# A Hymba block's up projection on one core: the weight rows read into buffers of half a row, each taken anew by itself, and the last stores put on three queues

## The chip, the core and the metric

One core of a Trainium2 chip runs the kernel. The metric is the device time of one launch in microseconds (us); smaller is better. The engines named below are PE (matrix products), DVE and ACT (elementwise work), POOL (here almost only an issuer of transfers) and SP (issues transfers and nothing else). Each engine works through its own instructions in a fixed order. An instruction whose inputs are not ready holds up everything behind it on that engine, and a transfer that must wait for its buffer holds up the transfers behind it on the same queue.

## The reference, cut to what matters

The block is one decoder layer on 512 tokens of width 2048: an input projection, two token mixers, an output projection, and then a gated feed-forward part. The change touches this last part and the final norm:

```
h = rmsnorm(x) * (1 + sc2) + sh2                       # 512 x 2048
u = h @ w_up                                           # 2048 -> 2 * 5632
y = conv_b + sum_j conv_w[j] * shifted(u, j)           # causal, width 3
val, gate = split(y)
x = x + gt2 * ((silu(gate) * val) @ w_down)
return rmsnorm(x)
```

## The kernel before

All large products are made in three passes (`mm3`, lines 118 to 122): each operand is split into a rounded part and a remainder, and hi*hi, hi*lo and lo*hi are added. For the weights, `wsplit` (line 845) does it on the fly: ACT casts 128x1024 numbers to the high part (line 850), and DVE subtracts to get the low part `ulo` (line 852). Three pairs of buffers are used in turn, so a cast may begin only when the product three places earlier has used its high part up.

**The steps of the up projection.** The 88 output tiles of 128 channels are taken as 44 pairs (a value tile and its gate tile), one pair a step `j`. The pair's weights are two rows of `wup`, 128x2048 each (1 MB). With the input channels cut in two, a row gives two parts: row `2j` is W11 and W12, row `2j+1` is W21 and W22. The activations are cut into two input halves and two token halves. Each step is then a product of two 2x2 block matrices and is made of seven block products of 24 matmuls each (128x128 by 128x256) in the place of eight. Their weights are, in the program's order:

| product | weight | activation tiles (PE rows) |
|---|---|---|
| 1 | w11 | y (Y11) |
| 2 | w12 | y (Y21) |
| 3 | r1 = W21 + W22 | t (T1) |
| 4 | r2 = r1 + w11 | t (T2) |
| 5 | r4 = r2 + w12 | y (Y22) |
| 6 | r3 = W11 + W21 | t (T3) |
| 7 | w22 | t (T4), made a step later |

DVE makes `r2` and `r4` by additions (lines 1022 and 1030). `r1` and `r3` are made by transfers: SP loads one addend, and POOL then issues an accumulating transfer that adds the other on top (lines 995 and 998). `r2`, `r3` and `r4` use the three `wide` buffers.

**The order of the steps.** For the first ten pairs, products 1 and 2 were already made ahead of the loop (`first_two`) and stored in `early`. The loop goes 10, 0, 11, 1, ..., 19, 9 and then 20 to 43. A step with `j >= 10` makes seven products on PE (its own first six, and product 7 of the step before); I call it a full step. A step with `j < 10` (`NB` in the code) makes five; I call it a short step. So the first twenty steps are ten pairs of a full and a short step with 12 products, and the last 24 are full steps.

**The row buffers.** Four buffers of 1 MB (tags `x2_0` to `x2_3`) hold the rows. Every step takes two of them, and two steps later they are taken again:

```python
w.append(row(2 * j + i, rb, f"x2_{(0, 2, 1, 3)[rows % 4]}"))
...
w11, w12, r1, w22 = w[0][:, W1], w[0][:, W2], w[1][:, W1], w[1][:, W2]
G.dma_start(r1, a["wup"][2 * j + 1, :, W2], accum_op=ALU.add)
```

A row is one tile and is loaded by one transfer of 1 MB (line 865). The second row holds W21, on which `r1` is accumulated, and W22, whose product is made only in the following step; the tile is given back when both have been read.

**What sets the order on the engines.** The program is written in the order above, but a scheduler then places the instructions of each engine. For the trace it is its placing that counts.

**The end.** After the down projection, the last residual gives a norm over the second 256 tokens. Four blocks of 128x4x256 (512 KB each) are multiplied by it and stored (`finish`, line 1132): the first on POOL, the other three on DVE, and all four stores stand on SP's queue, the first block's ahead.

Of the kernel before, what the change touches and what calls it, by code (L numbers as in the profile page):

```python
# [9 lines left out]
F32 = mybir.dt.float32  # L10
# [6 lines left out]
P = 128  # L17
# [9 lines left out]
NB = 10  # L27
# [28 lines left out]
def block_kernel(ctx, tc, a, out, stop=None, dbg=None):  # L56
    nc = tc.nc
    V, S, G, PE = nc.vector, nc.scalar, nc.gpsimd, nc.tensor
# [118 lines left out]
    if True:  # L177
# [9 lines left out]
        rstd = p0.tile([P, T], F32, tag="rs0", name="rs0")  # L187
# [18 lines left out]
        for k in range(KT):  # L206
            for part in (1, 0):
                j = part * 16 + k
                wa = p0.tile([P, D], F32, tag="wa", name="wa", bufs=4)
# [405 lines left out]
    def start_pair(p):  # L615
        if p:
            rkv = []
            for i in range(3):
                t = vtile("v") if i == 2 else ring("rkv")
                nc.sync.dma_start(t, sp[p, i])  # L620
                rkv.append(t)
        else:
            rkv = rkv0
        return stage_a(p, rkv)
# [5 lines left out]
    with hp():  # L630
        q = start_pair(0)
        stage_b(0, q)
    win_pair(1)
    for p in range(NP):
# [5 lines left out]
        with hp():  # L640
            stage_c(p, q)
            if p + 1 < NP:
                stage_b(p + 1, qn)
                q = qn
# [51 lines left out]
    rb = ctx.enter_context(tc.tile_pool(name="rb", bufs=1, reuse_waits="tile"))  # L696
    psm = ctx.enter_context(tc.tile_pool(name="psm", bufs=8, space=PSUM, reuse_waits="tile"))
    HT = T // 2
    H0, H1 = slice(0, HT), slice(HT, T)
    QW = 4 * P  # L700

    def bank():
        return psm.tile([P, T], F32, tag="b", name="b")
# [5 lines left out]
    def wide(name):  # L709

        return rb.tile([P, 4, HT], F32, tag="wide", name=name, bufs=3)
# [31 lines left out]
    def norm_rows(acc):  # L743
        pst = bank()
        rms_stats(pst, acc)
        return rms_rows(rb, pst, HT // P)

    def norm_bcast(dg):
        psb = bank()
        rms_bcast(psb, dg, HT // P)  # L750
        return psb[:, 0:HT]
# [52 lines left out]
    for f in range(8, KT):  # L804
        if f == 9:
            dg = norm_rows(acc[:, H0])
        if f == 10:
            rstd = norm_bcast(dg)
# [46 lines left out]
    def product(ps, w, Y, start=True):  # L855
        wh, wl = wsplit(w)
        for k in range(8):
            sl = slice(k * P, (k + 1) * P)
            y = Y[k // 4]
            mm3(ps, wh[:, sl], wl[:, sl], y[:, 0, k % 4, :], y[:, 1, k % 4, :], start=start and k == 0,  # L860
                stop=k == 7, more=not start)

    def row(n, pool, tag):
        t = pool.tile([P, 4 * QW], F32, tag=tag, name="wrow")
        nc.sync.dma_start(t, a["wup"][n, :, :])
        return t

    W1, W2 = slice(0, 2 * QW), slice(2 * QW, 4 * QW)
# [42 lines left out]
    for n in range(NB):  # L911
# [3 lines left out]
        if n == 1:  # L915
            rstd = norm_bcast(dg)
# [21 lines left out]
    def finish_pair(j, u1, u2):  # L938
        yv, yg = Slot("yv"), Slot("yg")
        conv(u1.t, yv.t, col("cw", j), col("cw", 88 + j), col("cw", 176 + j), col("cb", j))  # L940
        u1.done()

        conv(u2.t, yg.t, ncw[:, 0, j : j + 1], ncw[:, 1, j : j + 1], ncw[:, 2, j : j + 1], col("cb", 44 + j))
        u2.done()
        S.activation(yg.t, yg.t, AF.Silu)
        V.tensor_mul(yv.t, yv.t, yg.t)
        yg.done()
        nc.sync.dma_start(ad[j], yv.t)
        yv.done()
# [4 lines left out]
    def act_pair(i):  # L954

        pool, tag = ATAGS[i % len(ATAGS)]
        t = pool.tile([P, 2, 2, T], F32R, tag=tag, name="act2")
        for n in range(2):
            s_ = Slot("al")
            nc.sync.dma_start(s_.t, ad[2 * i + n])  # L960
            S.copy(t[:, 0, n, :], s_.t)
            V.tensor_tensor(t[:, 1, n, :], s_.t, t[:, 0, n, :].bitcast(F32), op=ALU.subtract)
            s_.done()
        return [(t[:, 0, n, :], t[:, 1, n, :]) for n in range(2)]
# [3 lines left out]
    def ahead_of_down(j):  # L968
        if j == NF - 1:
            A.extend(act_pair(len(A) // 2))  # L970

    pend = None

    def last_product(p):

        j, u1, u2, b, w22, x = p
        product(b, w22, T4, start=False)
        if x is None:
            S.copy(u2[:, H0], b)
        else:  # L980
            V.tensor_add(u2[:, H0], x[:, H0], b)
            x.done()
        finish_pair(j, u1, u2)


    order = [j for n in range(NB) for j in (NB + n, n)] + list(range(2 * NB, NF))
    rows = 0
    for j in order:
        w = []
        for i in range(2):  # L990
            w.append(row(2 * j + i, rb, f"x2_{(0, 2, 1, 3)[rows % 4]}"))
            rows += 1

        w11, w12, r1, w22 = w[0][:, W1], w[0][:, W2], w[1][:, W1], w[1][:, W2]
        G.dma_start(r1, a["wup"][2 * j + 1, :, W2], accum_op=ALU.add)
        r3 = wide("r3").rearrange("p a b -> p (a b)")
        nc.sync.dma_start(r3, a["wup"][2 * j, :, W1])
        G.dma_start(r3, a["wup"][2 * j + 1, :, W1], accum_op=ALU.add)
        pa = bank()[:, 0:HT]
        cap = Slot("cap")  # L1000
        if j < NB:
            u1 = Slot("u1")
            nc.sync.dma_start(u1.t, early[j])
            if pend:
                last_product(pend)
        else:
            product(pa, w11, Y11)
            S.copy(cap[:, H0], pa)
            if pend:
                last_product(pend)  # L1010
            u1 = Slot("u1")
            pb = bank()[:, 0:HT]
            product(pb, w12, Y21)
            V.tensor_add(u1[:, H0], cap[:, H0], pb)
        ahead_of_down(j)
        u2 = Slot("u2")
        pc = bank()[:, 0:HT]
        product(pc, r1, T1)
        S.copy(cap[:, H1], pc)
        ahead_of_down(j)  # L1020
        r2 = wide("r2").rearrange("p a b -> p (a b)")
        V.tensor_add(r2, r1, w11)
        product(pa, r2, T2, start=j < NB)
        if j < NB:
            V.tensor_add(cap[:, H0], u1[:, H1], pa)
        else:
            S.copy(cap[:, H0], pa)
        ahead_of_down(j)
        r4 = wide("r4").rearrange("p a b -> p (a b)")
        V.tensor_add(r4, r2, w12)  # L1030
        product(pc, r4, Y22, start=False)
        V.tensor_add(u1[:, H1], cap[:, H0], pc)
        ahead_of_down(j)
        if j < NB:
            pd = bank()[:, 0:HT]
            product(pd, r3, T3)
            V.tensor_add(u2[:, H1], cap[:, H0], cap[:, H1])
            V.tensor_add(u2[:, H1], u2[:, H1], pd)
            pend = (j, u1, u2, pd, w22, cap)
        else:  # L1040
            product(pa, r3, T3, start=False)
            V.tensor_add(u2[:, H1], cap[:, H1], pa)  # L1042
            cap.done()
            pend = (j, u1, u2, pa, w22, None)
# [84 lines left out]
        residual(f, ps, gate(f), acc, lo, hi, f == 0)  # L1129
        S.activation(x2(f, slice(lo, hi)), x2(f, slice(lo, hi)), AF.Identity, bias=eps[:, 2:3], scale=col("nf", f))  # L1130

    def finish(hs, q, rstd, eng=V):
        x = x2q[q][:, :, hs]
        eng.tensor_tensor(x, x, rstd[:, None, :].to_broadcast([P, 4, HT]), op=ALU.mult)
        nc.sync.dma_start(out[:, 4 * q : 4 * q + 4, hs], x)

    for f in range(NWF):
        if f == 0:
# [9 lines left out]
    for f in range(NWF, KT):  # L1148
        n = f - NWF
        if n == 1:  # L1150
            dg = norm_rows(acc[:, H0])
        if n == 2:
            rstd = norm_bcast(dg)
        if n >= 3 and n < 7:
            finish(H0, n - 3, rstd)
        down_half(1, f)
    rstd = norm_bcast(norm_rows(acc[:, H1]))
    rs = Slot("rs")
    S.copy(rs[:, H0], rstd)
    finish(H1, 0, rs[:, H0], G)  # L1160
    for q in range(1, 4):
        finish(H1, q, rstd)


def pack(x, c, w_ada, b_ada, norm1_g, w_in, mu_shift, w0, w2, a0, a2, g2, k_k, k_a, r_k, ln_x_w, ln_x_b,
# [95 lines left out]
```

## Time and profile before

| | us |
|---|---|
| median of 3 runs | 2437.19 (2434.59 to 2441.55) |
| the profiled execution's own time | 2435.95 |
| its span, from the first to the last instruction | 2434.2 |
| PE busy | 2299.5 (94% of the span) |
| DVE busy | 1643.5 (68%) |
| ACT busy | 1058.0 (43%) |
| mean clock granted to PE | 0.982 |

In the profile's rows, a line such as L852 is a line of the kernel, `out<-in` names the tiles with their numbers left out (`wrow` is a weight row, `r` any of r2, r3 and r4, `u` a result), and `x` is a count. The bracket at the end of a row is how long the engine stood idle just before it and what it was waiting for. A row of SPq or POOL with DMA_DIRECT2D is the issue of a transfer, not the transfer itself. PEclk is the clock granted to PE as a share of its full one, and DMA is the mean busy share of the core's 16 transfer engines. The up projection's loop lies between about 1040 and 1900 us of the span, and its ten pairs of steps end near 1440.

### The profile page before, as it was taken

Reading aid. Unit: us, or ns where it says so; the run is one execution under the profiler, and the core shown is the slowest. Engines: PE = TensorE matmul, PEld = TensorE weight load, DVE = VectorE, ACT = ScalarE, POOL = GpSimd, SP = SyncE. Lnnn points to the kernel's source line nnn. Section 1 sums busy time; section 2 is a strip of 40 time slices with the busy share of each in tenths; the row PEclk is TensorE's granted clock in tenths of the full one; section 3 lists DMA queues with packets and bytes.
Section 4 is the critical chain, followed back from the end, with each engine's and each line's share of the span. In section 5 each row is a group of like instructions: output and inputs, shape, how many; then the busy total and the mean of one; then the engine's idle time right before and its main releaser. Section 6 shows DMA issues by size and latency. Waiting matters only on the chain.

```text
span 2434.2 us, 42678 instructions
## 1 busy us (share of the span) xinstructions
PE 2299.5 (94%) x17122; PEld 1990.3 (82%) x17122; DVE 1643.5 (68%) x2623; ACT 1058.0 (43%) x1491; POOL 127.0 (5%) x184
## 2 busy tenths in 40 slices
PE   4789999999999999999989899999999999999997
PEld 3656666667666789999989899999999988888897
DVE  6987777777774456776767677777777735353354
ACT  3234344443433346644444445555555622233353
POOL 0000000000000010011010000000001000110000
PEclk9999999999999999999999999999999999999998
DMA  9976665556572756677676777677777857764465
GB/s 343 340 230 164 169 166 152 166 168 176 166 209 74 251 180 185 219 225 208 201 204 201 207 199 196 197 200 202 200 199 203 255 172 280 249 205 119 115 181 162
DMA packets 213946, 483.06 MB, mean 198 GB/s; under 512 B 73137, under 2 KB 78705, under 8 KB 194289
## 3 DMA queue, kind: packets, MB, share of 16 engines
q1 hardware_dynamic: 195026, 414.77, 52.4%
q0 software_dynamic: 18720, 65.55, 13.1%
q8 instruction: 134, 2.20, 0.4%
q14 instruction: 66, 0.54, 0.1%
HBM read 441.70 MB, written 38.54 MB: 197 GB/s over the span
## 4 chain that ended last, share of the span: by engine, by line
PE 73%; DMA 10%; DVE 9%; issue 3%; ACT 3%; SPq 1%; DVEq 0%; POOLq 0%; ACTq 0%
PE b L122 17%; PE b L120 17%; PE b L121 17%; DMA wrow<-wup 7%; PE mm L120 3%; PE mm L121 3%; PE mm L122 3%; DVE jk L212 3%; DVE ulo L852 2%; PE pb L537 1%; PE pb L535 1%; DMA war<-ada 1%; PE pb L528 1%; DMA wraw<-win 1%; DVE wlo L115 1%
## 5 line engine op out<-in xcount | busy, mean ns | idle before, releaser
L122 PE MATMUL b<-t,ulo 128*128 128x256 f32 x1408 | 403.5, 288 | 34.3 <-DVE ulo L852 34.3
L120 PE MATMUL b<-t,uhi 128*128 128x256 f32 x1408 | 403.5, 287 | 0.9 <-DVE u L1042 0.9
L121 PE MATMUL b<-t,uhi 128*128 128x256 f32 x1408 | 402.3, 286 | 0.0
L122 PE MATMUL b<-act,ulo 128*128 128x512 f32 (+1 forms) x880 | 308.0, 350 | 0.0
L121 PE MATMUL b<-act,uhi 128*128 128x512 f32 (+1 forms) x880 | 307.8, 350 | 0.0
L120 PE MATMUL b<-act,uhi 128*128 128x512 f32 (+1 forms) x880 | 307.6, 350 | 0.0
L122 PEld LDWEIGHTS b<-t,ulo 128*128 128x128 f32 x1408 | 272.4, 194 | 36.9 <-DVE ulo L852 36.9
L120 PE MATMUL b<-y,uhi 128*128 128x256 f32 x1056 | 299.1, 283 | 1.0 <-ACT uhi L850 1.0
L122 PE MATMUL b<-y,ulo 128*128 128x256 f32 x1056 | 298.5, 283 | 0.7 <-DVE ulo L852 0.7
L121 PE MATMUL b<-y,uhi 128*128 128x256 f32 x1056 | 298.5, 283 | 0.0
L850 ACT CAST uhi<-wrow 128x1024 fp32r<-128x1024 f32 x176 | 184.4, 1048 | 226.9 <-PE b L121 214.8
L852 DVE TENSOR_TENSOR ulo<-wd,uhi 128x1024 fp32r<-128x1024 f32 (+1 forms) x120 | 136.3, 1135 | 215.8 <-ACT uhi L850 215.0
L120 PEld LDWEIGHTS b<-t,uhi 128*128 128x128 f32 x1408 | 272.8, 194 | 2.4 <-DVE u L1042 1.3
L121 PEld LDWEIGHTS b<-t,uhi 128*128 128x128 f32 x1408 | 272.6, 194 | 0.0
L113 ACT CAST whi<-wraw 128x512 fp32r<-128x512 f32 x236 | 145.6, 619 | 286.4 <-PE mm L121 114.3
L852 DVE TENSOR_TENSOR ulo<-wrow,uhi 128x1024 fp32r<-128x1024 f32 x176 | 214.7, 1222 | 69.8 <-ACT uhi L850 69.8
L850 ACT CAST uhi<-wd 128x1024 fp32r<-128x1024 f32 (+1 forms) x120 | 117.4, 978 | 292.4 <-PE b L121 290.7
L115 DVE TENSOR_TENSOR wlo<-wraw,whi 128x512 fp32r<-128x512 f32 x236 | 161.4, 688 | 113.9 <-ACT whi L113 101.3
L852 DVE TENSOR_TENSOR ulo<-r,uhi 128x1024 fp32r<-128x1024 f32 x132 | 161.1, 1220 | 72.7 <-ACT uhi L850 72.4
L850 ACT CAST uhi<-r 128x1024 fp32r<-128x1024 f32 x132 | 138.6, 1050 | 161.6 <-PE b L121 160.1
L120 PEld LDWEIGHTS b<-y,uhi 128*128 128x128 f32 x1056 | 201.5, 191 | 1.4 <-ACT uhi L850 1.4
L122 PEld LDWEIGHTS b<-y,ulo 128*128 128x128 f32 x1056 | 200.8, 190 | 1.1 <-DVE ulo L852 1.1
(310 smaller groups left out, 4706.3 us busy)
## 6 DMA issues: line engine op xcount, KB each, us to landing
wrow<-wup SPq DMA_DIRECT2D x98, 1024.0 KB, 5.3
wa<-ada SPq DMA_DIRECT2D x48, 1024.0 KB, 7.1
war<-ada SPq DMA_DIRECT2D x192, 256.0 KB, 3.5
wd<-wdn SPq DMA_DIRECT2D x80, 512.0 KB, 4.0
wraw<-win SPq DMA_DIRECT2D x140, 256.0 KB, 4.2
wraw<-wout SPq DMA_DIRECT2D x96, 256.0 KB, 3.5
wrow<-wup POOLq DMA_DIRECT2D x44, 512.0 KB, 5.7
r<-wup SPq DMA_DIRECT2D x44, 512.0 KB, 4.6
```

What stands on the lines that cost most here:

```text
L113: S.copy(hi, raw)
L115: eng.tensor_tensor(lo, raw, hi[:, :].bitcast(F32), op=ALU.subtract)
L120: PE.matmul(ps, wh, xh, start=start, stop=False, skip_group_check=more)
L121: PE.matmul(ps, wh, xl, start=False, stop=False, skip_group_check=more)
L122: return PE.matmul(ps, wl, xh, start=False, stop=stop, skip_group_check=more)
L212: V.scalar_tensor_tensor(jk, wa, 1.0, cb, op0=ALU.mult, op1=ALU.mult, accum_out=mod[:, j : j + 1])
L528: PE.transpose(pst[:, i * P : (i + 1) * P], src[:, cl], ident)
L535: PE.matmul(pss[h][:, 0:128], bt[HS[h], cl], ar[HS[h], c, 1, :], start=True, stop=True)
L537: PE.matmul(pss[h][:, 128:384], kt[HS[h], cl], ar[HS[h], c, :, :], start=True, stop=True)
L850: S.copy(hi[:, 0:n], src)
L852: lo_of[0] = V.tensor_tensor(lo[:, 0:n], src, hi[:, 0:n].bitcast(F32), op=ALU.subtract)
```

## The change

The four buffers of 1 MB are taken once, ahead of the loop, and each is used as two halves; a half is a quarter of a step's weights, hence `wquart`. Each half is loaded by a transfer of its own, and waits only for the readers of its own earlier contents. The parts are paired anew: W21 (which becomes r1) shares a buffer with w11, and w12 one with w22. W21 is written first in the program. In a short step, product 7 of the step before is written after the product of r1 and no longer before it. Two of the last four stores go to ACT's queue, one to POOL's, and one stays with SP.

```diff
-    rows = 0
-    for j in order:
-        w = []
-        for i in range(2):
-            w.append(row(2 * j + i, rb, f"x2_{(0, 2, 1, 3)[rows % 4]}"))
-            rows += 1
-
-        w11, w12, r1, w22 = w[0][:, W1], w[0][:, W2], w[1][:, W1], w[1][:, W2]
+    wq = [rb.tile([P, 4 * QW], F32, tag=f"x2_{i}", name="wquart") for i in (0, 2, 1, 3)]
+    for n, j in enumerate(order):
+        wa, wb = wq[2 * (n % 2)], wq[2 * (n % 2) + 1]
+
+        r1, w11, w12, w22 = wa[:, W1], wa[:, W2], wb[:, W1], wb[:, W2]
+        nc.sync.dma_start(r1, a["wup"][2 * j + 1, :, W1])
         G.dma_start(r1, a["wup"][2 * j + 1, :, W2], accum_op=ALU.add)
+        nc.sync.dma_start(w11, a["wup"][2 * j, :, W1])
+        nc.sync.dma_start(w12, a["wup"][2 * j, :, W2])
+        nc.sync.dma_start(w22, a["wup"][2 * j + 1, :, W2])
         r3 = wide("r3").rearrange("p a b -> p (a b)")
         nc.sync.dma_start(r3, a["wup"][2 * j, :, W1])
         G.dma_start(r3, a["wup"][2 * j + 1, :, W1], accum_op=ALU.add)
...
         if j < NB:
             u1 = Slot("u1")
             nc.sync.dma_start(u1.t, early[j])
-            if pend:
-                last_product(pend)
...
         product(pc, r1, T1)
         S.copy(cap[:, H1], pc)
+        if j < NB:
+            last_product(pend)
...
-    def finish(hs, q, rstd, eng=V):
+    def finish(hs, q, rstd, eng=V, store=nc.sync):
         x = x2q[q][:, :, hs]
         eng.tensor_tensor(x, x, rstd[:, None, :].to_broadcast([P, 4, HT]), op=ALU.mult)
-        nc.sync.dma_start(out[:, 4 * q : 4 * q + 4, hs], x)
+        store.dma_start(out[:, 4 * q : 4 * q + 4, hs], x)
...
-    finish(H1, 0, rs[:, H0], G)
+    finish(H1, 0, rs[:, H0], G, G)
     for q in range(1, 4):
-        finish(H1, q, rstd)
+        finish(H1, q, rstd, V, (nc.sync, S)[q % 2])
```

The names in the rows below: `r2_13652`, `r3_13340` and so on are the buffers of one step; `yg`, `yv`, `cap` and `u1` are intermediate results of the convolution and of the sums. The step whose end the rows show is the short step `j = 6`; the next full step is `j = 17`.

On DVE, before, from the splitting of the short step's r2 to that of its r3 (step 6) and on:

```order
L852 TENSOR_TENSOR ulo_13422<-r2_13418,uhi_13420 128x1024
L852 TENSOR_TENSOR ulo_13453<-r4_13449,uhi_13451 128x1024
L933 SCALAR_TENSOR_TENSOR yg_13377<-u2_13213,ncw_10649,yg_13377 128x511
L1022 TENSOR_TENSOR r2_13652<-wrow_13513,wrow_13511 128x1024
L934 SCALAR_TENSOR_TENSOR yg_13377<-u2_13213,ncw_10649,yg_13377 128x510
L1025 TENSOR_TENSOR cap_13344<-u1_13345,b_13343 128x256
L852 TENSOR_TENSOR ulo_13483<-r3_13340,uhi_13481 128x1024
```

The addition L1022 makes r2 of step 17, and the splitting of step 6's own r3, for its last product, stands three rows behind it.

The same place on DVE, now:

```order
L852 TENSOR_TENSOR ulo_13426<-r2_13422,uhi_13424 128x1024
L852 TENSOR_TENSOR ulo_13457<-r4_13453,uhi_13455 128x1024
L1024 TENSOR_TENSOR r2_13656<-wquart_10695 128x1024
L852 TENSOR_TENSOR ulo_13487<-r3_13344,uhi_13485 128x1024
L933 SCALAR_TENSOR_TENSOR yg_13412<-u2_13217,ncw_10649,yg_13412 128x511
L1032 TENSOR_TENSOR r4_13687<-r2_13656,wquart_10696 128x1024
L934 SCALAR_TENSOR_TENSOR yg_13412<-u2_13217,ncw_10649,yg_13412 128x510
L1027 TENSOR_TENSOR cap_13348<-u1_13349,b_13347 128x256
L852 TENSOR_TENSOR ulo_13527<-wquart_10695,uhi_13525 128x1024
```

Step 17's addition (now L1024) still stands ahead of the splitting of step 6's r3, directly ahead of it, and step 17's r4 has moved up too, ahead of the splitting of its w11.

On SP's queue, before, from step 6's early result on (`wrow_13337` and `wrow_13513` are the second rows, W21 and W22, of steps 6 and 17, `wrow_13511` and `wrow_13743` the first rows of steps 17 and 7):

```order
L1003 DMA u1_13345<-early6_9926 128x512
L865 DMA wrow_13337<-wup 128x2048
L865 DMA wrow_13511<-wup 128x2048
L997 DMA r3_13340<-wup 128x1024
L948 DMA ad5_10656<-yv_13171 128x512
L865 DMA wrow_13743<-wup 128x2048
L865 DMA wrow_13513<-wup 128x2048
L997 DMA r3_13516<-wup 128x1024
L948 DMA ad16_10667<-yv_13376 128x512
```

The same stretch now (buffer 10695 holds r1 and w11 of the full steps, 10696 their w12 and w22; 10697 and 10698 hold those of the short ones; L993 loads W21, L995 w11, L996 w12 and L997 w22):

```order
L1005 DMA u1_13349<-early6_9926 128x512
L997 DMA wquart_10698<-wup 128x1024
L996 DMA wquart_10696<-wup 128x1024
L993 DMA wquart_10695<-wup 128x1024
L999 DMA r3_13344<-wup 128x1024
L948 DMA ad5_10656<-yv_13175 128x512
L995 DMA wquart_10697<-wup 128x1024
L996 DMA wquart_10698<-wup 128x1024
L993 DMA wquart_10697<-wup 128x1024
L997 DMA wquart_10696<-wup 128x1024
L999 DMA r3_13520<-wup 128x1024
L995 DMA wquart_10695<-wup 128x1024
```

The load of step 17's W21 (L993 into 10695) has moved from behind the store `ad5` to ahead of step 6's r3 load, while the load of its w22 (L997 into 10696) stays behind.

## The prediction

> **What bounds the kernel now.** I read the page's busy times first, then the loop's stretch in windows, then PE's waits there, and last one stall on each engine in order of time.
>
> ```profile
> span 2434.2 us, 42678 instructions
> ...
> PE 2299.5 (94%) x17122; PEld 1990.3 (82%) x17122; DVE 1643.5 (68%) x2623; ACT 1058.0 (43%) x1491; POOL 127.0 (5%) x184
> ```
>
> PE is busy for 94% of the span, so it is the bound, and the change touches only what PE loses in the loop and what lies behind its last product. The two halves of the loop, as windows (the columns are PE, PEld, DVE, ACT and POOL busy with their counts, then PEclk, DMA share, GB/s):
>
> ```profile
> 1040.00:1480.00 440.00, 404.81 (x3239) 400.90 (x3238) 317.47 (x376) 202.39 (x259) 40.46 (x47) 0.96 0.73 205
> 1480.00:1880.00 400.00, 400.00 (x3364) 400.00 (x3363) 304.17 (x341) 210.95 (x280) 35.00 (x40) 1.00 0.71 198
> ```
>
> The full steps at the end (second row) keep PE busy throughout: 400 / 3364 = 0.1189 us a matmul. At that rate the first row's 3239 matmuls, the ten pairs of steps in the main, take 385.1 us. They take 440, so **54.9 us are lost there**: 440 - 404.81 = 35.2 in which PE is idle, and 19.7 at a lower clock (PEclk 0.96). PE's waits in the loop, and three of the stalls (the bracket is the idle time just before):
>
> ```profile
> PE b L122 <- DVE ulo L852: 35.0, 15, 4.5
> ```
>
> ```profile
> 1079.04 0.38 PE L122 MATMUL b<-t,ulo 128*128 128x256 f32 x1 [3.83 <-DVE ulo L852]
> ...
> 1318.56 0.58 PE L122 MATMUL b<-t,ulo 128*128 128x256 f32 x1 [2.71 <-DVE ulo L852]
> ...
> 1436.62 0.39 PE L122 MATMUL b<-t,ulo 128*128 128x256 f32 x1 [3.27 <-DVE ulo L852]
> ```
>
> There are ten large stalls, of 2.5 to 4.5 us, one in each pair; (1436.62 - 1079.04) / 9 = 39.7 us is a pair's length. Always the same product stands: the short step's r3, whose low part comes late from DVE. DVE before the stall at 1318.56:
>
> ```profile
> 1309.40 1.23 DVE L852 TENSOR_TENSOR ulo<-r,uhi 128x1024 fp32r<-128x1024 f32 x1 [3.10 <-ACT uhi L850]
> 1310.55 0.74 DVE L933 SCALAR_TENSOR_TENSOR yg<-u,ncw,yg 128x511 f32<-128x511 f32 x1
> 1315.15 1.23 DVE L1022 TENSOR_TENSOR r<-wrow 128x1024 f32<-128x1024 f32 x1 [3.86 <-DMA wrow<-wup]
> 1316.29 0.74 DVE L934 SCALAR_TENSOR_TENSOR yg<-u,ncw,yg 128x510 f32<-128x510 f32 x1
> 1316.95 0.42 DVE L1025 TENSOR_TENSOR cap<-u,b 128x256 f32<-128x256 f32 x1
> 1317.29 1.22 DVE L852 TENSOR_TENSOR ulo<-r,uhi 128x1024 fp32r<-128x1024 f32 x1
> ```
>
> These are the rows of the order. DVE stands 3.86 us at the addition L1022 for step 17, until the accumulating transfer for that step's r1 has landed; the splitting that PE wants (1317.29) is queued behind. Its cast was long done:
>
> ```profile
> 1310.64 1.05 ACT L850 CAST uhi<-r 128x1024 fp32r<-128x1024 f32 x1
> ```
>
> Why r1 comes so late is seen on DVE and POOL:
>
> ```profile
> 1299.33 1.23 DVE L852 TENSOR_TENSOR ulo<-wrow,uhi 128x1024 fp32r<-128x1024 f32 x1 [0.30 <-ACT uhi L850]
> ```
>
> ```profile
> 1309.65 0.88 POOL L995 DMA_DIRECT2D wrow<-wup  x1 [11.64 <-DMA wrow<-wup]
> ```
>
> The buffer for step 17's second row holds step 16's w22 until the low part of it is made (1299.33 + 1.23 = 1300.56). Then a load of 1 MB runs, beside another, until about 1309.6, and the accumulating one until 1315.1: 14.6 us from release to landing. Of this buffer, the half that r1 needs was free much earlier (next part).
>
> The clock, in windows about the same stall (PE busy, PEclk, DMA share, GB/s):
>
> ```profile
> 1312.00:1316.00 4.00, 3.85 (x33) 1.00 1.00 185
> 1316.00:1320.00 4.00, 1.44 (x6) 0.81 0.32 65
> 1320.00:1324.00 4.00, 4.00 (x28) 0.76 0.59 158
> 1324.00:1328.00 4.00, 4.00 (x36) 1.00 0.79 268
> ```
>
> After the stall PE makes 28 matmuls in 4 us in the place of 36. Over the ten pairs this is the 19.7 us, about 2 a stall; it goes if the stalls go. [...]
>
> **The change part by part.** *Half buffers.* r1's half is now released by its own readers alone: the addition for r2, and the splitting for product 3. Before, for step 16, that splitting is
>
> ```profile
> 1287.92 1.23 DVE L852 TENSOR_TENSOR ulo<-wrow,uhi 128x1024 fp32r<-128x1024 f32 x1 [0.84 <-ACT uhi L850]
> ```
>
> and ends at 1289.15, 11.4 us ahead of the present release. What follows is a load of 512 KB and an accumulating one of 512 KB. Their times from issue to landing, first on the page, then in the worst stretch (1246 to 1252):
>
> ```profile
> wrow<-wup SPq DMA_DIRECT2D x98, 1024.0 KB, 5.3
> ...
> wrow<-wup POOLq DMA_DIRECT2D x44, 512.0 KB, 5.7
> r<-wup SPq DMA_DIRECT2D x44, 512.0 KB, 4.6
> ```
>
> ```profile
> wrow<-wup POOLq DMA_DIRECT2D x1, 512.0 KB, 9.3
> r<-wup SPq DMA_DIRECT2D x1, 512.0 KB, 8.0
> ```
>
> Between them I allow 0.5 us. So r1 lands 10.8 to 17.8 us after 1289.15: from 1299.9 to 1306.9. In the new order DVE reaches the addition where the split of 1309.40 has ended, about 1310.6, so it finds its data there with 3.7 to 10.7 us to spare, and the splitting of r3 behind it is done by 1310.6 + 2 x 1.23 = 1313.1. PE wants it at 1315.85 (1318.56 less the 2.71 of the bracket). **The stall goes**: 10 stalls, with their low clock.
>
> *What moves with it.* SP issues 88 transfers more (44 steps by two rows), since each 1 MB load becomes two of 512 KB; the bytes are the same. Its queue is in order, so I went through it for a pair: each load waits for a split or an addition which DVE makes in the same order as the loads stand, and none for a split later than the one before it by more than the ad store does. That store (row ad5) stood ahead of step 17's W21 and now stands behind it. On POOL, r1's and r3's transfers still alternate. Step 6's own r3, now queued there behind step 17's r1, is released as before:
>
> ```profile
> 1292.01 0.33 SPq L997 DMA_DIRECT2D r<-wup  x1
> ```
>
> With 10.8 to 17.8 us it lands at 1302.8 to 1309.8, before the cast at 1310.64: cost nothing, but the cover is thin in the worst case, and the cast could then slip 2 us more before PE stands.
>
> *Product 7 behind r1's product in a short step.* The count of matmuls is the same. r1 is needed one product (2.85 us) sooner, but its half is released by the short step before, a pair (39.7 us) ahead. w22's half is released one product later, and it is wanted a pair later. Nothing.
>
> *DVE.* A pair has 317.47 / 440 x 39.7 = 28.6 us of DVE work. Unstalled, a pair lasts 288 x 0.1189 = 34.2 us, so DVE would be 84% busy, against 76% in the later steps, where PE never waits for it. Two additions more stand among the short step's splits; they were there or just behind before.
>
> *What is left.* The group has fifteen waits, five more than the pairs; the transfers of 9.3 and 8.0 us above lie at one of the five, and with the half released 11.4 us sooner these should go too. I leave 3 us of the 54.9 standing for these, for the first pair, whose buffers still hang on the norm's results, and for what I don't see. Gain in the loop: **52 us** (bounds 27, if half of each loss stays, and 54.9).
>
> *The last stores.* DVE, POOL and SP at the end:
>
> ```profile
> 2423.60 3.48 DVE L1134 TENSOR_TENSOR x<-x,b 128x1024 f32<-128x1024 f32 x3 [1.78 <-ACT rs L1159]
> ```
>
> ```profile
> 2423.65 2.34 POOL L1134 TENSOR_TENSOR x<-x,rs 128x1024 f32<-128x1024 f32 x1 [189.22 <-ACT rs L1159]
> ```
>
> ```profile
> 2426.02 3.04 SPq L1135 DMA_DIRECT2D out<-x  x4
> ```
>
> ```profile
> 2426.00:2427.00 1.00, 0.00 (x0) 0.00 (x0) 1.00 (x1) 0.00 (x0) 0.00 (x0) 0.50 0.02 8
> 2427.00:2432.00 5.00, 0.00 (x0) 0.00 (x0) 0.09 (x1) 0.00 (x0) 0.00 (x0) 0.50 1.09 385
> ```
>
> POOL's block, at the head of SP's queue, holds up three blocks of which DVE has the first at 2424.8. From 2427.0 the transfers run at 385 GB/s without a gap. Now the first store can go 1.2 us sooner, and at 512 KB / 385 = 1.36 us each the next ones follow DVE's pace. No row shows a store on ACT's queue or at the end on POOL's; bounds are a gain of 1.4 (all stores ahead by what POOL holds up) and a loss of 1 (POOL's issue, 0.88 us in the rows above, on the path). I take a gain of **1.2**, nearest the row of 385 GB/s. [...]
>
> **The sum.** 2435.95 (the profiled execution, 1.24 below the median) - 52 - 1.2 = 2382.75, so 2383.
>
> **The rivals.** *DVE late in the short steps.* If the closer order leaves PE waiting 1 us a pair, each such stall costs its 1 us and 2 of low clock: 10 x 3 = 30, and the time is 2412. For it: 84%. Against it: 2.7 us in hand (1313.1 against 1315.85).
>
> *Another wait in the same place.* r3 lands after the cast's last moment (1312.6): its two transfers would have to take over 20 us. Then DVE stands as before, and the time is 2435. The same comes out if the loads of the halves still waited for w22, so that the change does not do what it says; W21's load standing ahead of w22's on SP speaks against that.
>
> *Slower: halves that don't overlap.* If the two halves of a row cost the transfer engines 2 x 4.6 - 5.3 = 3.9 us more, a pair has 0.73 x 39.7 = 29.0 us of transfer time and 4 x 3.9 = 15.6 more, 44.6, longer than now by 4.9; a later step has 0.71 x 168 x 0.1189 = 14.2 + 7.8 = 22.0, where it lasts 20.0. That is 10 x 4.9 + 24 x 2.0 = 97 more: 2532. It decides from some 2.7 us a row on. Against it: the four stores of 512 KB above, one behind the other at 385 GB/s. [...]
>
> **Chances.** The forecast 0.79, DVE late 0.12, another wait or no effect 0.06, slower 0.03. Under 0.3% (7.3 us) a measurement of this kernel can't tell from no change. Faster 0.91, same 0.06, slower 0.03. The range goes from 2376 (54.9 and 1.4 gained are 2379.65; the fastest run of before lies 2.6 below its median, and 1 more is left for waits that I don't see) to 2406, which takes in most of the second case.
>
> **What will show it.** Right: 1040 to 1440 at PEclk 0.99 or 1.00, no L122 wait above 1 us, pairs of 34 to 35 us, DMA share there near 0.84, L1024 without a wait for a transfer, and the last stores' traffic beginning near 2426 less the gain. Wrong: L852 of `r` still late behind L1024 (r1 too late), or behind its own cast (r3 too late), or DVE without gaps (DVE the bound); or PE gaps behind 1480, which would be the transfers.

## The result, and the profile after

The changed kernel takes 2383.21 us (median of 4 runs, 2379.27 to 2385.91) against 2438.64 (4 runs, 2434.59 to 2441.55): a ratio of 0.9773, 95% interval 0.9752 to 0.9793. The forecast was 2383. Its page, and the two windows and PE's waits (1000 to 1900) that were shown of before:

```profile
span 2384.1 us, 42898 instructions
...
PE 2278.3 (96%) x17122; PEld 1974.1 (83%) x17122; DVE 1643.4 (69%) x2623; ACT 1061.9 (45%) x1491; POOL 126.3 (5%) x185
```

```profile
1040.00:1480.00 440.00, 440.00 (x3700) 440.00 (x3699) 360.06 (x423) 234.47 (x298) 44.83 (x53) 1.00 0.84 232
1480.00:1880.00 400.00, 400.00 (x3338) 398.78 (x3337) 308.11 (x351) 217.22 (x292) 31.82 (x37) 1.00 0.75 204
```

```profile
PE b L120 <- ACT uhi L850: 2.8, 2, 2.6
PE b L122 <- DVE ulo L852: 0.5, 1, 0.5
```

In the stretch that held the ten pairs before (they now end some 50 us sooner) PE makes 3700 matmuls in 440 us where it made 3239, with no idle time and at the full clock; 440 / 3700 = 0.1189 us each, the rate of the last steps. What waits are left lie ahead of the first pair (the longest at 1030.85), while PE works on the last early rows. The stalled place on DVE, in the pair that matches the one shown of before (r1's splitting, then the addition that waited, and the splitting behind it):

```profile
1257.99 1.23 DVE L852 TENSOR_TENSOR ulo<-wquart,uhi 128x1024 fp32r<-128x1024 f32 x1 [1.12 <-ACT uhi L850]
...
1279.24 1.23 DVE L1024 TENSOR_TENSOR r<-wquart 128x1024 f32<-128x1024 f32 x1
1280.80 1.23 DVE L852 TENSOR_TENSOR ulo<-r,uhi 128x1024 fp32r<-128x1024 f32 x1 [0.33 <-ACT uhi L850]
```

```profile
1259.24 0.33 SPq L993 DMA_DIRECT2D wquart<-wup  x1
```

```profile
1264.26 0.86 POOL L994 DMA_DIRECT2D wquart<-wup  x1 [15.77 <-DMA wquart<-wup]
```

```profile
wquart<-wup POOLq DMA_DIRECT2D x1, 512.0 KB, 8.7
```

The splitting ends at 1259.22, SP issues the next W21 at 1259.24, POOL the accumulating transfer at 1264.26, and that one lands 8.7 us later, at 1273.0. DVE comes to the addition at 1279.24 and finds its data there with 6.3 us to spare. The splitting of r3 then waits only for its own cast and ends at 1282.03. PE's product of r3 begins at

```profile
1285.38 0.28 PE L120 MATMUL b<-t,uhi 128*128 128x256 f32 x1
1285.49 0.27 PE L121 MATMUL b<-t,uhi 128*128 128x256 f32 x1
1285.61 0.28 PE L122 MATMUL b<-t,ulo 128*128 128x256 f32 x1
```

and wants the low part at 1285.61: 3.6 us in hand where PE stood 2.5 to 4.5 us.

How much of the gain belongs to the change is best read past a mark that both kernels have: PE's second small product of the norm (L155), ahead of everything that was edited. Before, then after:

```profile
989.61 0.50 PE L155 MATMUL b<-cmat,acc 128*128 128x1 f32 x4
```

```profile
992.25 0.50 PE L155 MATMUL b<-cmat,acc 128*128 128x1 f32 x4
```

From there to the end of the span it was 2434.2 - 989.61 = 1444.6 us and is 2384.1 - 992.25 = 1391.85: 52.7 less. The 2.6 us by which the mark itself comes later are the part ahead of the edits, which differs by several microseconds from one execution of any of these kernels to the next (the mark lies between 985.4 and 994.2 in the executions below). I call the time behind the mark the stretch. Each is taken from one execution. Two executions of the changed kernel give 1391.9 and 1391.8, but the part of it ahead of the first pair can differ by 1.5 us between executions of the same loop (see best), so I build nothing on differences of the stretch under 2 us.

### The profile page after: what moved, and what is told of

Same layout as the page of the kernel before. It is cut to its first block, busy times and chain, and to the rows that moved or that the text cites. A ratio compares the mean times of both kernels' runs of the same rounds, so it can differ in the third digit from the quotient of the medians.

```text
span 2384.1 us, 42898 instructions
## 1 busy us (share of the span) xinstructions
PE 2278.3 (96%) x17122; PEld 1974.1 (83%) x17122; DVE 1643.4 (69%) x2623; ACT 1061.9 (45%) x1491; POOL 126.3 (5%) x185
## 4 chain that ended last, share of the span: by engine, by line
PE 82%; DVE 7%; DMA 5%; ACT 3%; issue 2%; SPq 0%; DVEq 0%; ACTq 0%
PE b L122 20%; PE b L120 20%; PE b L121 20%; PE mm L120 3%; PE mm L121 3%; PE mm L122 3%; DVE jk L212 3%; PE pb L537 1%; DMA wrow<-wup 1%; PE pb L535 1%; DMA war<-ada 1%; DMA wraw<-win 1%; PE pb L528 1%; DMA x<-dxz 1%; PE pa L298 1%
## 5 line engine op out<-in xcount | busy, mean ns | idle before, releaser
L122 PE MATMUL b<-t,ulo 128*128 128x256 f32 x1408 | 397.2, 282 | 0.0
L120 PE MATMUL b<-t,uhi 128*128 128x256 f32 x1408 | 396.8, 282 | 0.0
L121 PE MATMUL b<-t,uhi 128*128 128x256 f32 x1408 | 396.7, 282 | 0.0
L122 PE MATMUL b<-act,ulo 128*128 128x512 f32 (+1 forms) x880 | 308.0, 350 | 0.0
L122 PE MATMUL b<-y,ulo 128*128 128x256 f32 x1056 | 298.2, 283 | 0.5 <-DVE ulo L852 0.5
L120 PEld LDWEIGHTS b<-t,uhi 128*128 128x128 f32 x1408 | 266.9, 190 | 0.0
L122 PEld LDWEIGHTS b<-t,ulo 128*128 128x128 f32 x1408 | 266.9, 190 | 0.0
L121 PEld LDWEIGHTS b<-t,uhi 128*128 128x128 f32 x1408 | 266.8, 190 | 0.0
L850 ACT CAST uhi<-wquart 128x1024 fp32r<-128x1024 f32 x156 | 164.0, 1051 | 203.7 <-PE b L121 177.1
L852 DVE TENSOR_TENSOR ulo<-wquart,uhi 128x1024 fp32r<-128x1024 f32 x156 | 190.9, 1225 | 72.3 <-ACT uhi L850 72.3
L122 PEld LDWEIGHTS b<-y,ulo 128*128 128x128 f32 x1056 | 200.6, 190 | 0.7 <-DVE ulo L852 0.7
```

Of the source, the lines that this page charges most:

```text
L120: PE.matmul(ps, wh, xh, start=start, stop=False, skip_group_check=more)
L121: PE.matmul(ps, wh, xl, start=False, stop=False, skip_group_check=more)
L122: return PE.matmul(ps, wl, xh, start=False, stop=stop, skip_group_check=more)
L850: S.copy(hi[:, 0:n], src)
L852: lo_of[0] = V.tensor_tensor(lo[:, 0:n], src, hi[:, 0:n].bitcast(F32), op=ALU.subtract)
```

## The experiments

Each ratio is to the kernel before as timed on the same chip (medians 2436.62 to 2439.01 there); the row of before gives the first of these timings.

| kernel | median us | ratio to before, 95% | stretch us |
|---|---|---|---|
| before | 2438.64 | | 1444.6 |
| changed | 2383.21 | 0.9773 (0.9752 to 0.9793) | 1391.9 |
| last_only | 2408.85 | 0.9886 (0.9858 to 0.9914) | 1418.5 |
| after_no_last | 2381.21 | 0.9770 (0.9741 to 0.9800) | 1389.8 |
| whole_new_1mb | 2381.24 | 0.9774 (0.9748 to 0.9799) | 1392.3 |
| whole_old_half_loads | 2436.29 | 0.9996 (0.9982 to 1.0010) | 1448.3 |
| half_old | 2378.60 | 0.9758 (0.9726 to 0.9791) | 1389.5 |
| add_behind | 2388.66 | 0.9806 (0.9777 to 0.9836) | 1397.2 |
| stores_sp_last | 2378.43 | 0.9769 (0.9736 to 0.9802) | 1391.9 |
| stores_only | 2428.89 (one run) | | 1441.7 |
| stores_two | 2378.43 (one run) | | 1388.5 |
| after_again (the changed one) | 2381.07 | 0.9761 (0.9748 to 0.9774) | 1391.8 |
| best | 2376.59 | 0.9743 (0.9730 to 0.9757) | 1387.4 |

### Which part of the edit frees r1

**whole_old_half_loads**: the loads stay halves, W21 first, but whole buffers are taken anew and r1 shares one with w22 again.

```diff
-    wq = [rb.tile([P, 4 * QW], F32, tag=f"x2_{i}", name="wquart") for i in (0, 2, 1, 3)]
+    def take(n):
+        return [rb.tile([P, 4 * QW], F32, tag=f"x2_{i}", name="wquart") for i in ((0, 2), (1, 3))[n % 2]]
...
-        r1, w11, w12, w22 = wa[:, W1], wa[:, W2], wb[:, W1], wb[:, W2]
+        w11, w12, r1, w22 = wa[:, W1], wa[:, W2], wb[:, W1], wb[:, W2]
```

> The changed kernel with the old pairs (w11 with w12, r1 with w22) and each buffer taken anew as a whole every step, though still loaded by two transfers of 512 KB. Theory: r1's load waits for w22's splitting again; about 5.8 + 6.8 us of transfers and two DVE operations behind it against three products of cover: stalls of 3 to 5 us in each pair, 2430 to 2450. Rival (the smaller transfers, or W21 loaded first, carry the gain): no stall, 2384.

Measured 2436.29, no different from before. PE's waits are back, and DVE stands at the addition as it did (one of the longer ones):

```profile
PE b L122 <- DVE ulo L852: 34.9, 14, 5.1
```

```profile
1352.54 1.22 DVE L1026 TENSOR_TENSOR r<-wquart 128x1024 f32<-128x1024 f32 x1 [9.14 <-DMA wquart<-wup]
1353.68 1.22 DVE L852 TENSOR_TENSOR ulo<-r,uhi 128x1024 fp32r<-128x1024 f32 x1
```

So the smaller transfers, W21's load ahead and product 7's new place are together worth nothing while r1 is released with w22 and the addition stands ahead of r3's splitting (the second row) on DVE. Where the scheduler places the addition elsewhere, product 7's new place is worth something by itself (last_only, below).

**half_old**: halves taken one by one, as changed, but in the old pairs.

```diff
-        r1, w11, w12, w22 = wa[:, W1], wa[:, W2], wb[:, W1], wb[:, W2]
+        w11, w12, r1, w22 = wa[:, W1], wa[:, W2], wb[:, W1], wb[:, W2]
```

> The changed kernel with halves taken anew one by one, but in the old pairs (w11 with w12, r1 with w22). Theory: r1's half still has a release of its own, by its own splitting, so the pairs don't matter: no stall, 2383, within 4. Rival (the pairing is what frees r1): 2437.

**whole_new_1mb**: whole buffers of 1 MB taken anew, one transfer each, but in the new pairs.

```diff
+        w11, r1, w12, w22 = wa[:, W1], wa[:, W2], wb[:, W1], wb[:, W2]
+        for t, W in ((wa, W1), (wb, W2)):
+            nc.sync.dma_start(t.rearrange("p (i n) -> p i n", i=2), a["wup"][2 * j : 2 * j + 2, :, W].rearrange("i p n -> p i n"))
         G.dma_start(r1, a["wup"][2 * j + 1, :, W2], accum_op=ALU.add)
```

> The changed kernel with whole buffers of 1 MB, each taken anew every step and loaded by one transfer of 1 MB, but with the new pairs: W21 with w11 in one buffer, w12 with w22 in the other (a transfer takes the halves of two rows). Theory (what matters is only that r1 doesn't share its release with w22): r1's buffer is released by the same splitting as in the changed kernel, the load is longer by 1.5 to 3 us, and that is covered: no stall, 2384, within 5. Rival (the halves, taken anew one by one, are needed): the stall is back, 2425 to 2440.

Both lose all the stalls. Their windows, half_old first:

```profile
1040.00:1480.00 440.00, 440.00 (x3700) 440.00 (x3699) 359.64 (x423) 233.50 (x299) 44.97 (x53) 1.00 0.83 232
```

```profile
1040.00:1480.00 440.00, 440.00 (x3700) 440.00 (x3700) 359.80 (x423) 234.01 (x298) 44.74 (x53) 1.00 0.81 231
```

Either of two things is enough: halves with releases of their own, or the new pairs. They do the same: r1's load no longer waits for w22. The last window also prices the halves: for the same 3700 matmuls the transfer engines are busy 0.81 of the time with loads of 1 MB and 0.83 to 0.84 with halves, which is hidden here.

**after_no_last**: the changed kernel with product 7 back ahead of r1's product.

```diff
+            if pend:
+                last_product(pend)
...
-        if j < NB:
-            last_product(pend)
```

> The changed kernel with product 7 put back ahead of r1's product in the short steps. Theory: r1's half is released by its own splitting, one product (2.85 us) later than in the changed kernel, and the 3.7 to 10.7 us in hand cover that: no stall, 2384, within 4. Rival (the move carries part of the gain): waits of L122 on DVE's splitting come back, 1 us or more a pair with its half clock, 2400 to 2437.

2381.21: the move adds nothing to the halves.

### What a late r1 costs, and where

**last_only**: the kernel before with that move alone in place of all the rest.

```diff
             nc.sync.dma_start(u1.t, early[j])
-            if pend:
-                last_product(pend)
...
         S.copy(cap[:, H1], pc)
+        if j < NB:
+            last_product(pend)
```

> The kernel before with only product 7 moved behind r1's product in the short steps. On DVE this puts the splitting of the short step's r3 ahead of the addition L1022 that waits for r1; the addition then stands ahead of the next full step's w11. Theory (the release of the row buffer by w22's splitting is what is late): w22's splitting comes one product later, r1 lands one product later, and the same stall of 2.5 to 4.5 us moves to the next product (w11, tiles y in the place of t): 2437, within 10. Rival (the order on DVE is what makes PE stand): no stall is left, PE clock 1.00, 2384.

2408.85 lies between the two, and neither the theory nor the rival had it. The scheduler put the addition behind the splitting of r3 here, as the text above says, so the run changes the order on DVE too. The stall moved as the theory has it, to the next product (tile y), but it shrank. One of the ten pairs, the longest:

```profile
1261.23 0.39 PE L122 MATMUL b<-y,ulo 128*128 128x256 f32 x1 [2.10 <-DVE ulo L852]
1264.72 0.36 PE L120 MATMUL b<-t,uhi 128*128 128x256 f32 x1 [0.62 <-DVE u L1038]
```

SP's loads of the two rows and POOL's accumulating transfer in this pair of last_only, and SP's in the pair shown of before:

```profile
1242.72 2.93 SPq L865 DMA_DIRECT2D wrow<-wup  x2
```

```profile
1252.35 0.87 POOL L995 DMA_DIRECT2D wrow<-wup  x1 [11.44 <-DMA wrow<-wup]
```

```profile
1299.06 1.85 SPq L865 DMA_DIRECT2D wrow<-wup  x2
```

The second of two loads is issued 0.33 us before the row ends. Before, r1's 1 MB load went out at 1299.06 + 1.85 - 0.33 = 1300.58 and POOL took over at 1309.65: 9.1 us. In last_only it is 1245.32 to 1252.35: 7.0. Over all ten pairs that wait was 8.1 to 10.1 us before (mean 9.1) and is 5.3 to 7.0 in last_only (mean 6.0); from POOL's issue to PE's matmul both take about 9.0. So the load, issued at another moment, is 3 us shorter, and that is what my 2437 left out. In six pairs 0.3 to 0.6 us of the stall remains, in four 1.3 to 2.1, and some 0.6 behind it in nine (once 1.09). The pairs, in one window:

```profile
1040.00:1480.00 440.00, 421.72 (x3463) 415.37 (x3462) 332.11 (x398) 217.03 (x278) 41.80 (x49) 1.00 0.76 217
```

PE is idle for 440 - 421.72 = 18.3 us where it was 35.2, and loses 421.72 - 3463 x 0.1189 = 10.0 us by slower matmuls where it lost 19.7: 3.4 us of this window are at half clock (PEclk 0.50 from 1409.63 to 1413.05, in the last section), where the pairs had 37.5 us before. That the shorter load comes from less traffic beside it is likely, but not shown.

**add_behind**: the kernel before, with the late addition queued further back on DVE and nothing else touched.

```diff
-        V.tensor_add(r2, r1, w11)
+        if NB < j <= 2 * NB:
+            with tc.issue_after(r3lo.ins):
+                V.tensor_add(r2, r1, w11)
+        else:
+            V.tensor_add(r2, r1, w11)
...
             product(pd, r3, T3)
+            r3lo = lo_of[0]
```

> The kernel before, with one edit of order alone: on DVE the addition that makes r2 of a full step is queued behind the splitting of the short step's r3 (the scheduler then puts it behind the splitting of the full step's w11 too). Buffers, transfers and releases are as before, so r1 lands as late as before. Theory (a late r1 costs only what stands behind its addition on DVE): the next product behind the addition is the second of the next step, two products (5.7 us) further on than before, against stalls of 2.5 to 4.5: no stall of 1 us left, 2388, within 8. Rival (a late r1 is missed by the step itself, wherever the addition stands): the stall moves on, 2420 to 2440.

2388.66, as the theory had it:

```profile
PE b L122 <- DVE ulo L852: 3.9, 9, 0.8
PE b L120 <- DVE u L1047: 1.9, 5, 0.5
```

```profile
1319.29 1.22 DVE L852 TENSOR_TENSOR ulo<-wrow,uhi 128x1024 fp32r<-128x1024 f32 x1
1320.43 0.42 DVE L1042 TENSOR_TENSOR u<-cap 128x256 f32<-128x256 f32 x1
1320.85 1.22 DVE L1024 TENSOR_TENSOR r<-wrow 128x1024 f32<-128x1024 f32 x1
```

The addition stands behind the splitting of w11 and does not wait here; in seven of the pairs it still waits, for 7.8 us in all, without a stall of PE above 0.8 us. So 47 of the 53 us (1444.6 - 1397.2) could be had with the buffers and transfers as they were: PE never lacked r1; it lacked what was queued on DVE behind r1's first reader.

### The last stores

**stores_only**: the kernel before with only the last edit of the change.

```diff
-    finish(H1, 0, rs[:, H0], G)
+    finish(H1, 0, rs[:, H0], G, G)
...
-        finish(H1, q, rstd)
+        finish(H1, q, rstd, V, (nc.sync, S)[q % 2])
```

> The kernel before with only its last stores on three queues. Theory: the loop is as before (stalls of 2.5 to 4.5 us in ten pairs), and from the first of DVE's last blocks to the end of the span it is 10.6 us as in the changed kernel: 2437. Rival (the 1.2 us that was forecast): 9.4 us.

The stalls are there, 36.0 us of L122 waits, and from DVE's first of the last blocks (2416.51) to the end (2427.1) it takes 10.6 us, as before and as in the changed kernel. (Its one run lies 8 us below the median of before; of the 7.1 us between the two profiled spans, 4.2 lie ahead of the mark.) In the changed kernel the issues are

```profile
2373.53 3.48 DVE L1136 TENSOR_TENSOR x<-x,b 128x1024 f32<-128x1024 f32 x3 [1.78 <-ACT rs L1161]
2373.59 2.34 POOL L1136 TENSOR_TENSOR x<-x,rs 128x1024 f32<-128x1024 f32 x1 [189.71 <-ACT rs L1161]
2374.79 2.70 ACTq L1137 DMA_DIRECT2D out<-x  x2
2375.91 0.40 SPq L1137 DMA_DIRECT2D out<-x  x1
2376.22 0.80 POOL L1137 DMA_DIRECT2D out<-x  x1 [0.30 <-POOL x L1136]
```

The first store goes out 1.26 us behind DVE's start (2374.79) where it was 2.42 (2426.02 against 2423.60). The traffic of this stretch, in 40 slices from DVE's start to the end of the span, before and after:

```profile
GB/s 0 0 0 0 0 0 0 0 0 0 0 0 81 390 390 371 383 387 379 398 379 386 390 387 375 390 386 398 371 383 386 390 386 128 0 0 0 0 0 0
```

```profile
GB/s 0 0 0 0 0 0 0 0 178 376 380 388 395 384 376 388 388 399 372 399 422 388 461 388 345 376 380 388 345 23 0 0 0 0 0 0 0 0 0 0
```

A slice is 10.6 / 40 = 0.265 us. The bytes begin four slices sooner and end four sooner (by the transfers' own times the last byte is through 7.78 us behind DVE's start, where it was 8.96), but behind the last byte there are now 10 to 11 empty slices (2.84 us) where there were 6 to 7 (1.62).

**stores_sp_last**: all four on SP's queue, written with POOL's block last.

```diff
-    finish(H1, 0, rs[:, H0], G, G)
     for q in range(1, 4):
-        finish(H1, q, rstd, V, (nc.sync, S)[q % 2])
+        finish(H1, q, rstd)
+    finish(H1, 0, rs[:, H0], G)
```

> The changed kernel with the last four stores all on SP's queue again, but POOL's block stored last instead of first. From the first of DVE's last three blocks to the end of the span it was 10.60 us before and 10.57 in the changed kernel, though there the last byte came 1 us earlier. Theory (closing three queues in the place of one costs that 1 us): 9.5 us, the time 1 us below the changed kernel's, which the runs can't show and the profile can. Rival (the end doesn't hang on the queues): 10.6 us.

10.53 us, and it tells nothing of the question: the scheduler put POOL's block at the head of SP's queue again, and SP's first store went out 2.42 us behind DVE's start, as before.

**stores_two**: POOL's block stored from ACT's queue, DVE's three from SP's.

```diff
-    finish(H1, 0, rs[:, H0], G, G)
+    finish(H1, 0, rs[:, H0], G, S)
     for q in range(1, 4):
-        finish(H1, q, rstd, V, (nc.sync, S)[q % 2])
+        finish(H1, q, rstd)
```

> The changed kernel with the last stores on two queues: POOL's block on ACT's queue, DVE's three on SP's, none on POOL's. If it was the store on POOL's own queue that put the span's end 2.9 us behind the last byte instead of 1.7: 9.5 us from DVE's first block to the end. If any second queue does it: 10.6 us.

From 2367.21 to 2376.6 is 9.39 us: the 1.2 us are there once POOL's own queue carries no store. This run has one queue less as well, so it leaves open whether a third queue or POOL's costs the time; the traces decide it. Among the last instructions of each engine are DRAINs, put at the kernel's end (L1258; durations in ns, shortest, median and longest, then the first and the last start). In the changed kernel, then in stores_two:

```profile
L1258 POOLq DRAIN  x3: 46/93/7174, 2376.2 to 2383.9; - x3
L1258 SPq DRAIN  x3: 7/7/7, 2382.2 to 2383.6; - x3
```

```profile
L1258 POOLq DRAIN  x3: 46/102/6797, 2367.2 to 2376.4; - x3
L1258 SPq DRAIN  x3: 7/7/7, 2375.8 to 2376.1; - x3
```

In the changed kernel the last store lands at 2381.66 and SP is through its second DRAIN 0.57 us later, at 2382.23; in stores_two and before that takes 0.52, so three queues cost SP nothing. But POOL's long DRAIN lasts until 2376.20 + 7.17 = 2383.37, 1.1 us past SP's, and the span ends 0.78 us behind it. In stores_two it is over at 2374.02, ahead of SP's. Behind the last byte there are ten empty slices of 0.265 us in after_again, half_old and stores_only too, which have a store on POOL's queue, and six or seven (of 0.26 us in before and stores_sp_last, of 0.235 in best and stores_two) without one. So in the changed kernel the end hangs on POOL's DRAIN, which ends 2.7 us behind the landing of POOL's own store (2380.67); why it takes that long no run shows.

**best** and **after_again**: half_old with POOL's block really last on SP's queue, beside the changed kernel.

```diff
     for q in range(1, 4):
-        finish(H1, q, rstd, V, (nc.sync, S)[q % 2])
+        last = finish(H1, q, rstd)
+    with tc.issue_after(last.ins):
+        finish(H1, 0, rs[:, H0], G)
```

> half_old with the last four stores on SP's queue and POOL's block last there. From the first of DVE's last three blocks to the end: 9.5 us, if the span's end follows the last byte by 1.7 us where one queue stores, as it did before, and the bytes begin 1.1 us sooner; 10.6 us if the end hangs on something else. And the stretch from the norm's small product to the first product with a tile t, 64.6 us in the changed kernel, 62.2 as in half_old and before, if the old pairs are what keeps the first accumulating transfer from the last early weight rows; 64.6 if not. The time: 2379, 4 below the changed kernel's (rival: 2383).

> The changed kernel once more, on the same chip as the kernel of this call that is to beat it: 2383, within 3. From the norm's small product to the first product with a tile t 64.6 us again, if that is a property of the kernel; some 62 if it was chance.

The end takes 2380.4 - 2371.02 = 9.38 us, with SP's first store at 2372.27.

From the norm's small product to the first product with a tile t it is 60.7 us in best, 62.2 in half_old and before, 64.6 in both executions of the changed kernel, 64.7 in stores_sp_last and 63.0 in stores_two. So the changed kernel does pay some 2 us ahead of the first such product: there PE stands 2.6 us for an early row,

```profile
1030.85 0.58 PE L120 MATMUL b<-y,uhi 128*128 128x256 f32 x1 [2.63 <-ACT uhi L850]
```

whose load takes 10.1 us beside the first halves (7.0 in best), and the stall is followed by 6.83 us of half clock:

```profile
1030.32:1037.15 6.83, 6.14 (x27) 5.85 (x28) 5.83 (x6) 5.33 (x6) 0.13 (x1) 0.50 0.98 361
```

With this loop PE's waits in this part come to 3.0 to 3.4 us, with the old pairs to 1.7 or 1.8 (2.4 in last_only). The clock adds chance to it: in half_old and before 3.41 us of half clock fall here, and in best none, with the same waits. So the 1.5 us that best gains here on half_old, its own loop, are luck. In after_no_last the new pairs take 61.8, with a load of 8.6 us, waits of 2.5 and no half clock, so the pairs are not the whole of it; why the load is longer stays open. The stretch of best is 4.4 us shorter than the changed kernel's: 1.2 us at the end and 3.9 here, with 0.7 lost between the two. The medians say the same (2376.59 against 2381.07 on the same chip), though their intervals overlap. Best has the lowest ratio of this study, but not clear of half_old's.

## Why the prediction was right, point by point

- **54.9 us lost in the loop, by late splittings of r3.** Right. All of it went with r1's release, in every kernel whose r1 had a release apart from w22's, and none of it in whole_old_half_loads, where r1 had not. One reading was a little off: of the 19.7 us put down to the lower clock some 15 lie in the 37.5 us at half clock, behind eight of the ten stalls; the others are wider spacing of single matmuls beside the waits (0.18 to 0.25 us from one to the next in place of 0.119), at the full clock. The sum does not change by it.
- **Half buffers: r1 lands 10.8 to 17.8 us behind its release.** 13.7 in the pair shown (1259.22 to 1273.0). In hand at the addition 6.3 us (forecast 3.7 to 10.7), at PE 3.6 (forecast 2.7).
- **DVE 84% busy.** 360.06 / 440 = 82%, and PE never waited for it in this window. A pair lasts as forecast: first and last addition of nine pairs apart,

```profile
1073.60 1.23 DVE L1024 TENSOR_TENSOR r<-wquart 128x1024 f32<-128x1024 f32 x1
...
1382.06 1.22 DVE L1024 TENSOR_TENSOR r<-wquart 128x1024 f32<-128x1024 f32 x1
```

  (1382.06 - 1073.60) / 9 = 34.27 us, where 288 matmuls take 34.24. So "DVE late" did not come, nor did the transfers bind: their share is the 0.84 that was forecast.
- **3 us of waits left.** 3.3 (2.8 + 0.5), but all of it ahead of the first pair, on the early rows, where 1.7 stood before; in the pairs nothing is left. The reason given, that the first pair's own buffers come late, is not what the rows show.
- **Product 7's move: nothing.** Right beside the halves. What the prediction did not see is that by itself it is worth some 26 us (stretch 1418.5 against 1444.6), by a shorter load behind another order on DVE, and by less half clock (3.4 us where it was 37.5). It named one cure where three were open: release r1 sooner, load it faster, or queue its first reader further back.
- **The last stores: 1.2 us.** The step that failed. The wait went as described and the bytes ended 1.2 us sooner, but the price of a store on POOL's queue was taken as 0.88 us of issue at most, off the path. What it costs is 1.2 us behind the last byte (2.84 us to the end in place of 1.62), as POOL's DRAIN then ends last, so the term is 0: from DVE's first last block to the end it takes 10.6 us as before.
- **The sum.** 52 + 1.2 was forecast behind the mark, 52.7 was measured there: 55.1 us won between the first product with a tile t and the last blocks (1371.8 before, 1316.7 now), 2.4 lost ahead of that product (62.2 before, 64.6 now), nothing won at the end. The profiled execution then lost 2.6 us ahead of the mark by chance (2435.95 - 52.7 + 2.6 = 2385.9, its time), and the median of four runs lies 2.7 lower. These two, of opposite sign, nearly cancel, and so do 0.7 more in the loop's net gain than the 52 and the 1.2 that never came. That the number agrees to 0.2 us is luck; what the runs bear out is the loop's term.

## What to carry to other kernels

When an engine waits behind another's queue, ask three things: what the queue's head waits for, who holds that resource (here the last reader of the other half of the same buffer), and whether the head must stand there at all. Two tensors whose last readers lie far apart should not share one release; either giving each its own or pairing tensors that die together is enough. And sum a change over a stretch that begins at a mark both kernels share: here the mark itself moved by up to 9 us between executions, and the stretch leaves that out, though it too can differ by 1.5 us by chance.

## What the runs showed of the hardware that I had not expected

The granted clock after a stall did not follow from the stall's length. Before, it stayed at 1.00 after a gap of 3.50 us (ahead of 1238.25), and after one of 2.54 us (ahead of 1198.62) it averaged 0.68 up to 1204. In last_only it averaged 0.70 up to 1415 after a gap of 2.05 us (ahead of 1409.24), and stayed at 1.00 after one of 2.10 (ahead of 1261.23, shown above). The first and the third of these:

```profile
1238.25 0.39 PE L122 MATMUL b<-t,ulo 128*128 128x256 f32 x1 [3.50 <-DVE ulo L852]
```

```profile
1409.24 0.39 PE L122 MATMUL b<-y,ulo 128*128 128x256 f32 x1 [2.05 <-DVE ulo L852]
```

The clock behind the four gaps, before and then in last_only (PE busy first, with its matmuls, PEclk third from the end); the last row is the part at half clock of the row above it:

```profile
1238.25:1244.00 5.75, 5.75 (x48) 5.75 (x49) 5.75 (x9) 2.26 (x4) 0.00 (x0) 1.00 0.47 137
1198.62:1204.00 5.38, 5.38 (x32) 5.38 (x33) 5.10 (x8) 1.98 (x3) 0.00 (x0) 0.68 0.44 128
```

```profile
1261.23:1266.00 4.77, 4.15 (x33) 3.97 (x34) 4.77 (x8) 3.23 (x5) 0.00 (x0) 1.00 0.52 168
1409.24:1415.00 5.76, 5.75 (x35) 5.76 (x36) 5.76 (x9) 3.21 (x5) 0.00 (x0) 0.70 0.51 179
```

```profile
1409.63:1413.05 3.42, 3.42 (x18) 3.42 (x18) 3.42 (x7) 1.75 (x2) 0.00 (x0) 0.50 0.39 110
```

With PE busy for 5.75 us behind each, it makes 48 matmuls behind the gap of 3.50 us and 35 behind that of 2.05. Why the clock fell after the one gap and not after the other is not shown here.
